# Two-block network with a 64-expert layer, one core: output norm and stores placed ahead of the last expert set, whose 128 tokens are gathered, normed as one tile and scattered

## The chip, the cores and the metric

The kernel runs on one core of a Trainium2 chip, in one launch. Five engines take part, each with its own instruction stream that it works through in order: PE (matrix multiply), DVE (VectorE), ACT (ScalarE), POOL (GpSimd) and SP (SyncE, which here only issues DMAs). The metric is the device time of one execution in microseconds (us); lower is better. Matrix products write PSUM, which DVE and ACT read; everything else on the chip lies in SBUF.

## The reference, cut to what matters

The first block and the mixing half of the second block are untouched here. What matters is the end of the second block: a two-level mixture of experts over 1024 tokens of width 1024, added to the scaled input, and a layer norm.

```python
g_sel = top_k(x @ w_rg + b_rg, 1)                  # one group of 8 experts
top_v, top_i = top_k(logits of that group, 2)      # two experts of 64 for each token
weights = g_w * softmax(top_v)
ffn = sum over the token's two experts e of
      weight * ((silu(x @ w1[e]) * (x @ w3[e])) @ w2[e])      # w1, w3: 1024x512, w2: 512x1024
out = layer_norm(ALPHA * x + ffn, ln2_g, ln2_b)    # over the 1024 columns, eps 1e-5
```

## The kernel before, in words

The tokens of each expert are padded to a capacity and put into columns of 128 places. The experts are worked off in 30 sets (`ORDER`): a set of kind Q holds four experts of 32 places, S one expert of 128 places, and so on. The last three sets are 27 (S), 28 (S) and 29 (Q). For a set, `weights` issues the loads of its expert weights on SP's queue (three pieces of 2 MB for each expert: two halves of w1 and w3 together, then w2; for a Q set w2 comes in 16 loads of 512 KB, four for each expert), `hidden` forms pg and pu over eight steps of k and the product h (L1997 to L2005), and `rows` turns h, multiplies by w2 (py, L2022) and scales by the routing weight.

The weights stand in a ring of eight 2 MB buffers (`E.chunk`). A new load waits until the buffer's last reader is done. The last set needs 12 loads; its four w2 loads take the buffers of its own first four, so they can be issued only when the first half of its `hidden` (k of 0 to 3) has been multiplied.

For the sets up to 26 the rows of `rows` go out by an indirect DMA to y_d, two rows for each token. The last three sets are not stored: their rows are kept as a high and a low part (yh, yl, `split_scaled`, L183 and L184), and `spread` adds them to the 8 token tiles xr (128 tokens each, called K.xa in the code): a one-hot matrix S is made from the tokens' numbers (L2034), and for each tile two halves pa are multiplied from S, yh and yl (L2041, L2042) and added to xr by DVE (L2046). The spread of a set is worked in between the steps of the next set's `hidden`. The rows stored in y_d are fetched back by `add(c)` (L2098, four loads of two tiles, into four buffers of the same ring) and added to xr, the even tiles by DVE and the odd ones by POOL, two additions of 128x1024 each (L2102).

After the last set stands a loop, `further`, over experts that overflowed their capacity. Then the tail: the gain and bias of the norm are loaded as two rows broadcast to 128 partitions (L2136), and for each of the 8 tiles the spread of set 29 is multiplied, in most tiles with the tile itself added on PE through an identity (L2044), and the tile is normed in one of three ways (`LAST`, L2140 to L2166) that share the work between ACT, DVE and POOL, and stored on SP's queue (L2166). The recording layer orders each engine's instructions by its own plan; what it decided is shown below where the change speaks of it.

Of the kernel before, what the change touches and what calls it, by code (L numbers as in the profile page):

```python
# [27 lines left out]
NCOL = sum(CAP) // P  # L28
NOVF = 40
NLATE = 3  # L30
LAST = "qpfpffff"
# [1650 lines left out]
def route(tc, K, RT):  # L1682
# [207 lines left out]
    dve.tensor_copy(K.wtab, pw[:, :NC_])  # L1890


    K.nblk = RT("nblk", (1, 1), I32)
    dve.tensor_copy(K.nblk, oe[0:1, 63:64])
    e1, e2_ = N((64, 64)), N((64, 64))
    ec = ecol[:64]
    dve.tensor_scalar(e1, ob[:64], ec, None, op0=OP.is_le)
# [46 lines left out]
def experts(tc, I, K, out):  # L1944
# [64 lines left out]
    def rows(R, h, parts, w, between=lambda t, bank: None):  # L2009
# [18 lines left out]
        for j in range(2):  # L2028
            K.H.split_scaled(R[1][:, j], R[2][:, j], py[j], w)

    def spread(R, tok):

        S, yh, yl = R
        dve.tensor_scalar(S.rearrange("p a b -> p (a b)"), K.io, tok, None, op0=OP.is_equal)  # L2034

        def part(t, bank=PS, keep=False):
            o = S[:, t // 4, t % 4 * P:(t % 4 + 1) * P]
            ps = []
            for j in range(2):
                pa, x = bank("pa"), K.xa[t][:, hs[j]]  # L2040
                pe.matmul(pa, o, yh[:, j], start=True, stop=False)  # L2041
                pe.matmul(pa, o, yl[:, j], start=False, stop=not keep)  # L2042
                if keep:
                    pe.matmul(pa, ident, x, start=False, stop=True)  # L2044
                else:
                    dve.tensor_tensor(x, x, pa, op=OP.add)  # L2046
                ps.append(pa)
            return ps

        return part  # L2050

# [10 lines left out]

    col = lambda a, c: a[:, c:c + 1]

    def further():

        r = E.chunk(dt=F32R).rearrange("p (r a b) -> p r a b", a=2, b=512)
        r = [r[:, i] for i in range(3)]
        nb = nc.values_load(K.nblk[0:1, 0:1], min_val=0, max_val=NOVF)
        with tc.For_i(0, nb, 1) as it:  # L2070
            e = nc.sync.value_load(K.bexp[0:1, bass.ds(it, 1)], min_val=0, max_val=63)
            ix, fx = Z("ix", (P, 1), I32, bufs=1), Z("fx", (P, 2), bufs=1)
            for o, a in ((ix, K.xdx), (fx[:, 0:1], K.tokf), (fx[:, 1:2], K.wtab)):
                nc.sync.dma_start(o, a[:, bass.ds(it + NCOL, 1)])
            ws, = weights([e])
            parts = [(full, ws)]
            rows(r, hidden([turn(fetch(ix))], parts)[0], parts, fx[:, 1:2])
            add = spread(r, fx[:, 0:1])
            for t in range(8):
                add(t)  # L2080
# [1 line left out]
    def cols(rs):  # L2082
        return range(BASE[rs[0]] // P, BASE[rs[0]] // P + max(1, CAP[rs[0]] // P))

    nxt = lambda t, bank: None
# [7 lines left out]
    def add(c):  # L2093
# [5 lines left out]
        for j in range(2):  # L2099
            for k in range(2):  # L2100
                x = K.xa[2 * c + j]
                (dve, pool)[j].tensor_tensor(x, x, y[:, j, k], op=OP.add)  # L2102

    xs = K.xg
    xT = [turn(x, PS) for x in xs]
    for i, rs in enumerate(order):
        if i == len(order) - 1:
            for c in range(4):
                add(c)
        ws = weights(ids[i] if i < 2 else [expert_id(r) for r in rs], len(rs) in CUT)  # L2110
        n = P // len(rs)
        parts = [(slice(n * j, n * j + n), w) for j, w in enumerate(ws)]
        xs = [fetch(col(K.xdx, c)) for rs_ in order[i + 1:i + 2] for c in cols(rs_)]
        if i == 0:
            pool.memset(xg[1], 0.0)
            for t in range(8):
                pool.tensor_scalar(K.io[:, t * P:(t + 1) * P], K.io128, float(t * P), None, op0=OP.add)
            K.close_pool("q")
            E.grow()
        if i == n_late:  # L2120
            R = [S] + [K.A4(n, (P, 2, 512), F32R) for n in ("yh", "yl")]
        h = hidden(xT, parts, nxt)
        xT = [turn(x) for x in xs]
        for j, c in enumerate(cols(rs)):
# [12 lines left out]


    for t in range(8):
        x, kind = K.xa[t], LAST[t]  # L2140
        pa = nxt(t, (PS, PT)[t % 2], kind != "q")
        rv, rt = Z("zrv", (P, 1), bufs=2), Z("zrt", (P, 1), bufs=2)
        if kind == "f":
            sm, nm, ss = Z("zsm", (P, 2), bufs=2), Z("znf", (P, 1), bufs=2), Z("zss", (P, 1), bufs=2)
            for j in range(2):
                act.activation(x[:, hs[j]], pa[j], AF.Copy, accum_out=sm[:, j:j + 1])  # L2146
            dve.tensor_scalar(nm, sm[:, 0:1], sm[:, 1:2], -1.0 / D, op0=OP.add, op1=OP.mult)  # L2147
            act.activation(row[:, 2], x, AF.Square, bias=nm, accum_out=ss)  # L2148
            K.H.rstd_of(rv, ss, D, 1e-5, rt)
        else:  # L2150
            mv, nm, st = Z("zmv", (P, 2), bufs=2), Z("znm", (P, 1), bufs=2), Z("zst", (P, 2, 6), bufs=2)
            src = pa if kind == "p" else [x[:, h] for h in hs]
            for j in range(2):
                dve.bn_stats(st[:, j], src[j])
            dve.bn_aggr(mv, st)
            K.H.rstd_of(rv, mv[:, 1:2], 1, 1e-5, rt)
            dve.scalar_tensor_tensor(nm, mv[:, 0:1], -1.0, rv, op0=OP.mult, op1=OP.mult)
        if kind != "f":
            for j in range(2):
                act.activation(x[:, hs[j]], src[j], AF.Identity, scale=rv, bias=nm)  # L2160
            pool.tensor_tensor(x, x, row[:, 0], op=OP.mult)
            pool.tensor_tensor(x, x, row[:, 1], op=OP.add)
        else:
            dve.scalar_tensor_tensor(x, x, nm, row[:, 0], op0=OP.add, op1=OP.mult)  # L2164
            dve.scalar_tensor_tensor(x, x, rv, row[:, 1], op0=OP.mult, op1=OP.add)  # L2165
        nc.sync.dma_start(out[t * P:(t + 1) * P, :], x)  # L2166
    K.close_pool("e2")


# [64 lines left out]
```

## Time and profile before

| what | value |
|---|---|
| median of 3 runs | 3249.79 us (3246.05 to 3254.64) |
| the profiled execution | 3248.72 us |
| its span in the profile | 3246.8 us |
| busy share of the span: PE, DVE, ACT, POOL | 91%, 50%, 26%, 24% |
| HBM traffic over the span | 206 GB/s, in the expert phase about 420 GB/s |

The span is from the first to the last instruction that the profiler saw; the execution's own time is 1.9 us more, and the median is 1.1 us above that. Busy shares are means over stages with different limits, so the change is read from the last 130 us alone.

### The profile page before, as it was taken

The page shows a single profiled execution, that of the slowest core. Times are in us where ns is not written, and L with a number is a line of the kernel's source. Part 1 is how long each engine was busy: PE and PEld are TensorE (multiplying, and loading weights), DVE is VectorE, ACT ScalarE, POOL GpSimd, SP SyncE. Part 2 cuts the span into 40 slices and gives each one's busy share as a digit, 9 for nine tenths or more (in the row PEclk, how much of TensorE's full clock was granted, in tenths as well). Part 3 has the DMA queues.
Part 4 walks back from the last instruction along what each step waited for, and adds up shares of the span by engine and source line. Part 5 has one row for each costly group of instructions (what it writes and reads, how often), then busy time and mean ns, then how long its engine had stood idle before and what let it go on. Part 6 is the DMA issues. An engine that isn't in the chain of part 4 may idle for free. (4 is left out here: it accounts for less than half of the span.)

```text
span 3246.8 us, 39751 instructions
## 1 busy us (share of the span) xinstructions
PE 2970.0 (91%) x15247; PEld 2090.4 (64%) x15247; DVE 1635.0 (50%) x2700; ACT 847.3 (26%) x1474; POOL 768.1 (24%) x591
## 2 busy tenths in 40 slices
PE   7789989999999899999889999988989888989886
PEld 7789968888888678778778788963423322323232
DVE  7865495555566899885888544460000000000054
ACT  4233343333211533334332532120101100101002
POOL 4521174333200333333442142011000000000021
PEclk8899999999999899999999999988989999999998
DMA  3012222222622323313222575449999999999994
GB/s 122 18 45 100 79 78 79 88 87 97 240 88 91 117 91 105 110 67 109 66 62 71 175 238 174 170 195 414 390 422 396 422 416 414 427 400 425 386 426 190
DMA packets 135552, 656.54 MB, mean 202 GB/s; under 512 B 18693, under 2 KB 31877, under 8 KB 113728
## 3 DMA queue, kind: packets, MB, share of 16 engines
q1 hardware_dynamic: 119536, 615.75, 49.3%
q0 software_dynamic: 13520, 34.03, 2.7%
q10 hardware_dynamic: 2304, 4.20, 0.3%
q8 instruction: 121, 1.98, 0.3%
q14 instruction: 71, 0.58, 0.1%
HBM read 584.19 MB, written 85.46 MB: 206 GB/s over the span
## 5 line engine op out<-in xcount | busy, mean ns | idle before, releaser
L2005 DVE TENSOR_TENSOR h<-h,pu 128x512 f32<-128x512 f32 x32 | 22.0, 687 | 842.5 <-PE pu L1997 842.5
L1997 PE MATMUL pg<-w,xT 128*32 128x512 f32 (+2 forms) x1056 | 348.8, 633 | 76.7 <-DMA w<-in_we_dram 76.6
L1997 PE MATMUL pu<-w,xT 128*32 128x512 f32 (+2 forms) x1056 | 342.9, 622 | 0.0
L2022 PE MATMUL py<-w,hT 128*32 128x512 f32 (+2 forms) x1056 | 281.9, 599 | 15.5 <-issue 12.4
L1997 PEld LDWEIGHTS pg<-w,xT 128*32 128x32 f32 (+2 forms) x1056 | 96.0, 139 | 244.1 <-issue 128.3
L1997 PEld LDWEIGHTS pu<-w,xT 128*32 128x32 f32 (+2 forms) x1056 | 104.0, 140 | 168.9 <-issue 166.2
L2022 PEld LDWEIGHTS py<-w,hT 128*32 128x32 f32 (+2 forms) x1056 | 98.6, 135 | 166.8 <-issue 141.6
L321 POOL TENSOR_TENSOR ws<-wr 128x512 f32<-128x512 f32 x74 | 115.2, 1561 | 274.6 <-DMA wr<-in_w2T_dram 137.5
L1111 DVE TENSOR_TENSOR x<-x,pd 128x512 f32<-128x512 f32 x176 | 118.2, 685 | 76.2 <-PE pd L190 75.4
L180 DVE TENSOR_TENSOR ol<-ws,oh 128x512 fp32r<-128x512 f32 x148 | 123.6, 836 | 45.7 <-ACT oh L179 38.8
L2004 ACT ACTIVATE h<-pg 128x512 f32<-128x512 f32 x32 | 19.1, 597 | 484.9 <-PE pg L1997 462.0
L1678 POOL DMA_INDIRECT y_d<-y,ydx x29 | 29.0, 999 | 433.5 <-ACT y L2026 433.5
L179 ACT ACTIVATE oh<-ws 128x512 fp32r<-128x512 f32 x148 | 92.1, 626 | 141.0 <-PE pm L189 131.0
L1672 POOL DMA_INDIRECT xg<-x_d,xdx x31 | 31.6, 1020 | 402.5 <-PE pxg L1984 401.4
L189 PE MATMUL pd<-wdl,aoh 128*128 128x512 f32 x320 | 124.1, 392 | 0.0
L190 PE MATMUL pd<-wdh,aol 128*128 128x512 f32 x320 | 123.9, 391 | 0.0
L188 PE MATMUL pd<-wdh,aoh 128*128 128x512 f32 x320 | 121.5, 396 | 2.1 <-DVE b21l L184 2.1
L180 DVE TENSOR_TENSOR ol<-wr,oh 128x512 fp32r<-128x512 f32 x117 | 108.3, 927 | 5.1 <-ACT oh L179 2.8
L179 ACT ACTIVATE oh<-wr 128x512 fp32r<-128x512 f32 x117 | 72.9, 625 | 118.9 <-PE pm L189 110.0
L180 POOL TENSOR_TENSOR wl<-wrB,wh 128x512 fp32r<-128x512 f32 x40 | 60.0, 1522 | 181.8 <-ACT wh L179 181.8
L1213 DVE SCALAR_TENSOR_TENSOR cadve<-cadve,vec 128x512 f32<-128x512 f32 x105 | 102.1, 972 | 0.1
L1213 DVE SCALAR_TENSOR_TENSOR cudve<-cudve,vec 128x512 f32<-128x512 f32 x105 | 98.2, 936 | 0.8
(814 smaller groups left out, 7993.4 us busy)
## 6 DMA issues: line engine op xcount, KB each, us to landing
w<-in_we_dram SPq DMA_DIRECT2D x160, 2048.0 KB, 23.9
w<-in_we_dram SPq DMA_DIRECT2D x128, 512.0 KB, 10.3
wr<-in_w2T_dram SPq DMA_DIRECT2D x34, 512.0 KB, 4.1
wr<-in_wg_dram SPq DMA_DIRECT2D x22, 512.0 KB, 3.3
wr<-in_wu_dram SPq DMA_DIRECT2D x22, 512.0 KB, 4.1
act_d<-go SPq DMA_DIRECT2D x22, 512.0 KB, 2.9
wrD<-act_d SPq DMA_DIRECT2D x22, 512.0 KB, 3.3
wrD<-in_wd_dram SPq DMA_DIRECT2D x22, 512.0 KB, 4.4
```

The lines of the kernel that those rows point to most:

```text
L179: act.activation(hi, src, AF.Copy)
L180: (eng or dve).tensor_tensor(lo, src, hi.bitcast(F32), op=OP.subtract)
L188: pe.matmul(ps, l[0], r[0], start=(k == 0), stop=False)
L189: pe.matmul(ps, l[0], r[1], start=False, stop=False)
L190: pe.matmul(ps, l[1], r[0], start=False, stop=(k == n - 1))
L321: self.pool.tensor_tensor(s, self.s[a], self.s[b], op=op)
L1111: dve.tensor_tensor(xs, xs, pd, op=OP.add)
L1213: dve.scalar_tensor_tensor(o, x, w, c, op0=OP.mult, op1=OP.add)
L1672: nc.gpsimd.indirect_dma_start(out=x, out_offset=None, in_=K.x2d, in_offset=bass.IndirectOffsetOnAxis(ap=ix, axis=0), bounds_check=T - 1, ...
L1678: nc.gpsimd.indirect_dma_start(out=K.y2d, out_offset=bass.IndirectOffsetOnAxis(ap=ix, axis=0), in_=y, in_offset=None, bounds_check=2 * T - ...
L1997: pe.matmul(p[r], x[:, k, r], ws[k4][:, k % 4, j], start=(k == 0), stop=(k == 7))
L2022: pe.matmul(py[j][r], hT[:, k, r], ws[2][:, k, j], start=(k == 0), stop=(k == 3))
```

## The change

The sets, the routing and the weights stay. What moves is everything behind the last two sets.

- The spread of set 28 is no longer worked in between the steps of set 29's `hidden`. It runs in one piece right behind set 28's `rows`, in PSUM banks of both kinds in turn.
- Set 29 is not spread. Ahead of its `hidden`, its one-hot matrix S is turned on PE (pst, eight 128x128), and the finished token tiles are gathered by it on PE into px: 16 products of 128x512 in float32. A matrix `same` says which of the 128 places hold the same token. Behind set 29's `rows`, yh and yl times `same` are added to px (four products), and px is normed as one tile and scattered to the output by an indirect DMA on POOL's queue.
- All 8 tiles are normed (`norms`): statistics for four tiles at a time on DVE, then for each tile one pass on ACT into one of two buffers xg, a product with the gain on DVE, a sum with the bias on POOL and a store on POOL's queue. In the code this stands ahead of set 29's `hidden`. The tiles' rows that belong to set 29's tokens are overwritten by the scatter.
- Gain and bias (`row_load`) are loaded on SP's queue behind the loads of set 29's weights, into the buffers of K.io and of a turned input.
- `further` stands behind the scatter; a second loop, which runs at most once, repeats the spread of set 29 and the norms if there were overflowing experts.

```diff
+    def norms(ts):
+
+        n = len(ts)
+        mv = Z("zmv", (P, n, 2), bufs=2)
+        for i, t in enumerate(ts):
+            st = Z("zst", (P, 2, 6), bufs=2)
+            for j in range(2):
+                dve.bn_stats(st[:, j], K.xa[t][:, hs[j]])
+            dve.bn_aggr(mv[:, i], st)
+        rv, nm = Z("zrv", (P, n), bufs=2), Z("znm", (P, n), bufs=2)
+        K.H.rstd_of(rv, mv[:, :, 1], 1, 1e-5, Z("zrt", (P, n), bufs=2))
+        dve.scalar_tensor_tensor(nm, mv[:, :, 0], -1.0, rv, op0=OP.mult, op1=OP.mult)
+        for i, t in enumerate(ts):
+            o = xg[t % 2]
+            act.activation(o, K.xa[t], AF.Identity, scale=rv[:, i:i + 1], bias=nm[:, i:i + 1])
+            dve.tensor_tensor(o, o, row[0], op=OP.mult)
+            pool.tensor_tensor(o, o, row[1], op=OP.add)
+            nc.gpsimd.dma_start(out[t * P:(t + 1) * P, :], o)
...
+        if last:
+
+            tok = col(K.tokf, cols(rs)[0])
+            one_hot(R[0], tok)
+            row = [K.io, xTs[turned[0] % 2].rearrange("p k t -> p (k t)")]
+            row_load()
+            same = Z("same", (P, P), F32R)
+            ST = []
+            for j in range(2):
+                pq = PT("pst")
+                for t in range(4):
+                    pe.transpose(pq[:, t * P:(t + 1) * P], S[:, j, t * P:(t + 1) * P].bitcast(F32), ident)
+                ST.append(Z("h", (P, 512), bufs=2))
+                act.activation(ST[j], pq, AF.Copy)
...
+            px = [PS("px") for _ in range(2)]
+            for t in range(8):
+                for j in range(2):
+                    pe.matmul(px[j], ST[t // 4][:, t % 4 * P:(t % 4 + 1) * P], K.xa[t][:, hs[j]], start=(t == 0), stop=False)
+            norms(range(4))
+            norms(range(4, 8))
         h = hidden(xT, parts, nxt)
+        nxt = none
         xT = [turn(x) for x in xs]
+        if last:
+            act.activation(Z("zsq", (P, 1)), tok, AF.Sqrt)
...
-                nxt = spread(R, col(K.tokf, c))
-    further()
-    row = E.chunk().rearrange("p (a d) -> p a d", d=D)
-    for i in range(2):
-        nc.sync.dma_start(row[:, i], bass.AP(tensor=I["rows4"].tensor, offset=i * D, ap=[[0, P], [1, D]]))
...
+                if not last:
+                    nxt = spread(R, col(K.tokf, c))
+        if i == len(order) - 2:
+            for t in range(8):
+                nxt(t, (PS, PT)[t % 2])
+            nxt = none
+
+
+    st, mv, rv = Z("lst", (P, 2, 6)), Z("lmv", (P, 2)), Z("lrv", (P, 1))
+    for j in range(2):
+        for y in R[1:]:
+            pe.matmul(px[j], same, y[:, j], start=False, stop=(y is R[2]))
+        dve.bn_stats(st[:, j], px[j])
+    dve.bn_aggr(mv, st)
+    x = xg[1]
+    for j in range(2):
+        dve.scalar_tensor_tensor(x[:, hs[j]], px[j], mv[:, 0:1], row[0][:, hs[j]], op0=OP.subtract, op1=OP.mult)
+    K.H.rstd_of(rv, mv[:, 1:2], 1, 1e-5, Z("lrt", (P, 1)))
+    for j in range(2):
+        dve.scalar_tensor_tensor(x[:, hs[j]], x[:, hs[j]], rv, row[1][:, hs[j]], op0=OP.mult, op1=OP.add)
+    nc.gpsimd.indirect_dma_start(out=out, out_offset=bass.IndirectOffsetOnAxis(ap=col(K.xdx, cols(order[-1])[0]), axis=0), in_=x, in_offset=None,
+                                 bounds_check=T - 1, oob_is_err=False)
```

Where DVE's order changes first: before, around the end of set 28's `hidden`. L2046 adds a spread half from PSUM, L2102 a fetched row, L2005 is the product h of set 28, L184 its low part yl, L2034 a one-hot matrix.

```order
L2046 TENSOR_TENSOR xr<-xr,pa 128x512 x4
L2102 TENSOR_TENSOR xr<-xr,w 128x1024 x2
L2046 TENSOR_TENSOR xr<-xr,pa 128x512 x2
L2005 TENSOR_TENSOR h<-h,pu 128x512
L2046 TENSOR_TENSOR xr<-xr,pa 128x512 x2
L2034 TENSOR_SCALAR S<-io,tokf 128x1024
L2016 COPY hT<-ph 128x256
L2017 COPY hT<-ph 128x256
L2102 TENSOR_TENSOR xr<-xr,w 128x1024 x4
L184 SCALAR_TENSOR_TENSOR yl<-py,wtab,yh 128x512 x2
L2046 TENSOR_TENSOR xr<-xr,pa 128x512 x16
L2034 TENSOR_SCALAR S<-io,tokf 128x1024
```

The same place on DVE now, with the line numbers of the changed file (L2052 was L2046, L2106 was L2102, L2038 was L2034, L183 was L184).

```order
L2052 TENSOR_TENSOR xr<-xr,pa 128x512 x14
L2005 TENSOR_TENSOR h<-h,pu 128x512
L2052 TENSOR_TENSOR xr<-xr,pa 128x512 x2
L2038 TENSOR_SCALAR S<-io,tokf 128x1024
L2016 COPY hT<-ph 128x256
L2017 COPY hT<-ph 128x256
L2164 COPY xg_18956<-tokf 128x128
L183 SCALAR_TENSOR_TENSOR yl<-py,wtab,yh 128x512 x2
L2052 TENSOR_TENSOR xr<-xr,pa 128x512 x16
L2106 TENSOR_TENSOR xr<-xr,w 128x1024 x8
L2038 TENSOR_SCALAR S<-io,tokf 128x1024
L2119 BN_STATS zst<-xr 128x6 x3
```

All eight additions of fetched rows now stand behind the sixteen of set 28's spread, where before all eight stood ahead of them, and the one-hot matrix of set 29 stands behind all of these.

On PE the steps of set 29's `hidden` (pg and pu with 32 rows) began right behind set 28's py, with pieces of the spread between them; before:

```order
L2022 MATMUL py<-w,hT 128x512 x8
L1997 MATMUL pg<-w,xT_19273 32x512
L1997 MATMUL pu<-w,xT_19273 32x512
L2041 MATMUL pa<-yh,S 128x512
L2042 MATMUL pa<-yl,S 128x512
L2041 MATMUL pa<-yh,S 128x512
L2042 MATMUL pa<-yl,S 128x512
```

On PE now, from the end of set 28's spread on:

```order
L2050 MATMUL pa<-yh,S 128x512
L2051 MATMUL pa<-yl,S 128x512
L2160 MATMUL pst<-ident,S 128x128 x8
L2166 MATMUL ptok<-ident,xg_18956 128x128
L2171 MATMUL px<-xr,h 128x512 x16
L1997 MATMUL pg<-w,xT_19274 32x512 x4
L1997 MATMUL pu<-w,xT_19274 32x512 x4
L1997 MATMUL pg<-w,xT_19274 32x512 x4
```

Set 29's `hidden` now stands behind the whole spread, the eight turns of S and the sixteen gathering products.

On DVE behind the last set's rows stood, before, the end of set 29 and the entry of the loop:

```order
L2005 TENSOR_TENSOR h<-h,pu 128x512
L2016 COPY hT<-ph 128x256
L2017 COPY hT<-ph 128x256
L184 SCALAR_TENSOR_TENSOR yl<-py,wtab,yh 128x512 x2
L2069 TENSOR_LOAD nblk
L2070 COMPARE_AND_BRANCH
```

On DVE now, from the yl of set 29 on; L2127 is the product of a normed tile with the gain, L2199 the statistics of px:

```order
L183 SCALAR_TENSOR_TENSOR yl<-py,wtab,yh 128x512 x2
L2127 TENSOR_TENSOR xg_18956<-xg_18956,io 128x1024
L2127 TENSOR_TENSOR xg_19273<-xg_19273,io 128x1024
L2199 BN_STATS lst<-px 128x6 x2
L2200 BN_AGGR lmv<-lst 128x2
L193 TENSOR_SCALAR lrt<-lmv 128x1
L196 RECIPROCAL lrv<-rsq 128x1
L197 TENSOR_TENSOR rsq<-lrv 128x1
L198 TENSOR_TENSOR rsq<-rsq,lrt 128x1
L199 TENSOR_SCALAR rsq<-rsq 128x1
L200 TENSOR_TENSOR lrv<-lrv,rsq 128x1
L2127 TENSOR_TENSOR xg_18956<-xg_18956,io 128x1024
```

Five more of L2127 follow, and then the four passes over px (L2203, L2206). So none of the eight products with the gain stands ahead of set 29's last rows. On SP the two loads of gain and bias stand behind all 24 loads of set 29.

## Rows read from the trace of the kernel before

**Rows 1.** Windows: stretches in us, then busy time (instructions) by engine, clock, DMA.

```profile
core 0: us, PE busy (x) PEld busy (x) DVE busy (x) ACT busy (x) POOL busy (x), PEclk, DMA share, GB/s
3120.00:3140.00 20.00, 16.44 (x50) 8.71 (x49) 17.60 (x16) 0.60 (x1) 15.69 (x6) 1.00 1.02 429
...
3220.00:3247.00 27.00, 4.23 (x13) 2.07 (x11) 22.31 (x46) 9.87 (x26) 8.85 (x4) 0.64 0.35 140
```

**Rows 2.** Timeline of SP's queue, 3040 to 3205: start, us, line, transfer.

```profile
3119.11 32.97 SPq L1937 DMA_DIRECT2D w<-in_we_dram  x8
3174.02 14.91 SPq L1967 DMA_DIRECT2D w<-in_we_dram  x16
3202.62 0.82 SPq L2136 DMA_DIRECT2D w<-in_rows_dram  x2
```

**Rows 3.** Waits of SP's queue, 3040 to 3250: total us, times, longest.

```profile
SPq L1967 <- PE pu L1997: 30.1, 4, 21.8
```

**Rows 4.** Timeline of all engines around set 28, 3120 to 3152.

```profile
3133.02 5.99 DVE L2102 TENSOR_TENSOR xr<-xr,w 128x1024 f32<-128x1024 f32 x2
3135.58 1.02 PE L1997 MATMUL pu<-w,xT 128*128 128x512 f32 x2
3140.12 0.67 DVE L2005 TENSOR_TENSOR h<-h,pu 128x512 f32<-128x512 f32 x1
3143.05 7.13 PE L2022 MATMUL py<-w,hT 128*128 128x512 f32 x16 [0.88 <-DVE hT L2016]
3151.55 0.74 DVE L184 SCALAR_TENSOR_TENSOR yl<-py,wtab,yh 128x512 fp32r<-128x512 f32 x1
```

**Rows 5.** The lines L2102 and L2046: ns minimum/median/maximum of one, first and last start.

```profile
L2102 POOL TENSOR_TENSOR xr<-xr,w x8: 2357/3001/3327, 3121.7 to 3144.9; 128x1024 f32<-128x1024 f32 x8
L2102 DVE TENSOR_TENSOR xr<-xr,w x8: 1211/2702/3431, 3124.2 to 3150.4; 128x1024 f32<-128x1024 f32 x8
L2046 DVE TENSOR_TENSOR xr<-xr,pa x34: 673/686/690, 3117.7 to 3204.7; 128x512 f32<-128x512 f32 x34
```

**Rows 6.** Timeline of PE, ACT and DVE: a cold start, set 29's first half, float32 products, one-hot.

```profile
3090.56 1.91 PE L1997 MATMUL pg<-w,xT 128*128 128x512 f32 x2 [3.00 <-DMA w<-in_we_dram]
3095.80 1.02 PE L1997 MATMUL pg<-w,xT 128*128 128x512 f32 x2
3141.56 0.60 PE L2013 MATMUL ph<-ident,h 128*128 128x128 f32 x4
3141.92 0.74 DVE L2034 TENSOR_SCALAR S<-io,tokf 128x1024 fp32r<-128x1024 f32 x1
3167.78 1.07 PE L1997 MATMUL pg<-w,xT 128*32 128x512 f32 x8
3173.81 1.10 PE L1997 MATMUL pu<-w,xT 128*32 128x512 f32 x8
```

**Rows 7.** Timeline at the end of set 29 and the start of the tail.

```profile
3200.62 1.61 DVE L184 SCALAR_TENSOR_TENSOR yl<-py,wtab,yh 128x512 fp32r<-128x512 f32 x2 [15.87 <-ACT yh L183]
3202.96 0.50 PE L2041 MATMUL pa<-yh,S 128*128 128x512 f32 x1 [2.24 <-DVEq L2070]
```

**Rows 8.** Lines of ACT and POOL, a store's issue last: ns minimum/median/maximum.

```profile
L2148 ACT ACTIVATE w<-xr,znf x5: 1139/1147/1149, 3214.4 to 3237.6; 128x1024 f32<-128x1024 f32 x5
L2162 POOL TENSOR_TENSOR xr<-xr,w x3: 2349/2362/2370, 3215.7 to 3232.4; 128x1024 f32<-128x1024 f32 x3
L1659 POOL DMA_DIRECT2D x_d<-xr x8: 531/532/630, 2097.3 to 2151.7; - x8
```

**Rows 9.** DMA issues: queue, count, KB each, median us to landing; stores on POOL's queue first.

```profile
x_d<-xr POOLq DMA_DIRECT2D x8, 512.0 KB, 2.9
out_dram<-xr SPq DMA_DIRECT2D x8, 512.0 KB, 2.6
y_d<-y,ydx POOLq DMA_INDIRECT x7, 10.5
```

**Rows 10.** The last instruction that the timeline of the tail shows.

```profile
3243.00 0.33 SPq L2166 DMA_DIRECT2D out_dram<-xr  x1
```

More of the change, by code (lines that the diff above doesn't have):

```diff
@@ L1890, in route @@
     dve.tensor_copy(K.wtab, pw[:, :NC_])
[L1893 to L1894 removed]
+    K.nblk = RT("nblk", (1, 2), I32)
+    dve.tensor_copy(K.nblk[:, 0:1], oe[0:1, 63:64])
+    dve.tensor_scalar(K.nblk[:, 1:2], oe[0:1, 63:64], 1.0, None, op0=OP.min)
     e1, e2_ = N((64, 64)), N((64, 64))
@@ L2029, in rows, with places, one_hot, part @@
             K.H.split_scaled(R[1][:, j], R[2][:, j], py[j], w)
+    def places(again=True):
+        if again:
+            nc.sync.dma_start(K.io[:, 0:P], I["cmoe"][:, 8:8 + P])
+        for t in range(again, 8):
+            pool.tensor_scalar(K.io[:, t * P:(t + 1) * P], K.io[:, 0:P] if again else K.io128, float(t * P), None, op0=OP.add)
+    def one_hot(S, tok):
+        dve.tensor_scalar(S.rearrange("p a b -> p (a b)"), K.io, tok, None, op0=OP.is_equal)
     def spread(R, tok):
         S, yh, yl = R
-        dve.tensor_scalar(S.rearrange("p a b -> p (a b)"), K.io, tok, None, op0=OP.is_equal)
-        def part(t, bank=PS, keep=False):
+        if tok is not None:
+            one_hot(S, tok)
+        def part(t, bank=PS):
             o = S[:, t // 4, t % 4 * P:(t % 4 + 1) * P]
-            ps = []
             for j in range(2):
@@ L2041, in part @@
                 pe.matmul(pa, o, yh[:, j], start=True, stop=False)
[L2042 to L2048, printed above, removed]
+                pe.matmul(pa, o, yl[:, j], start=False, stop=True)
+                dve.tensor_tensor(x, x, pa, op=OP.add)
         return part
@@ L2083, in cols @@
         return range(BASE[rs[0]] // P, BASE[rs[0]] // P + max(1, CAP[rs[0]] // P))
-    nxt = lambda t, bank: None
+    none = nxt = lambda t, bank: None
     ids = [[expert_id(r) for r in rs] for rs in order[:2]]
@@ L2102, in add, with row_load @@
                 (dve, pool)[j].tensor_tensor(x, x, y[:, j, k], op=OP.add)
+    def row_load():
+        for k in range(2):
+            nc.sync.dma_start(row[k], bass.AP(tensor=I["rows4"].tensor, offset=k * D, ap=[[0, P], [1, D]]))
+    def norms(ts):
[15 more added lines that the diff above has]
+            nc.gpsimd.dma_start(out[t * P:(t + 1) * P, :], o)
     xs = K.xg
@@ L2106, in experts @@
     for i, rs in enumerate(order):
-        if i == len(order) - 1:
+        last = i == len(order) - 1
+        if last:
             for c in range(4):
@@ L2115, in experts @@
             pool.memset(xg[1], 0.0)
-            for t in range(8):
-                pool.tensor_scalar(K.io[:, t * P:(t + 1) * P], K.io128, float(t * P), None, op0=OP.add)
+            places(False)
             K.close_pool("q")
@@ L2121, in experts @@
             R = [S] + [K.A4(n, (P, 2, 512), F32R) for n in ("yh", "yl")]
+        if last:
[11 more added lines that the diff above has]
+                act.activation(ST[j], pq, AF.Copy)
+            tb = xg[0][:, 0:P]
+            dve.tensor_copy(tb, tok.to_broadcast([P, P]))
+            pq = PT("ptok")
+            pe.transpose(pq[:, 0:P], tb, ident)
+            dve.tensor_scalar(same, pq[:, 0:P], tok, None, op0=OP.is_equal)
+            px = [PS("px") for _ in range(2)]
[4 more added lines that the diff above has]
+            norms(range(4, 8))
         h = hidden(xT, parts, nxt)
+        nxt = none
         xT = [turn(x) for x in xs]
+        if last:
+            act.activation(Z("zsq", (P, 1)), tok, AF.Sqrt)
         for j, c in enumerate(cols(rs)):
@@ L2131, in experts @@
                 rows(R, h[j], parts, col(K.wtab, c), *[nxt] * (j > 0))
-                nxt = spread(R, col(K.tokf, c))
-    further()
-    row = E.chunk().rearrange("p (a d) -> p a d", d=D)
-    for i in range(2):
-        nc.sync.dma_start(row[:, i], bass.AP(tensor=I["rows4"].tensor, offset=i * D, ap=[[0, P], [1, D]]))
[L2139 to L2166, printed above, removed]
@@ L2167, in experts @@
+    further(nb)
+    with tc.For_i(0, nr, 1):
+        places()
+        add = spread(R, tok)
+        for t in range(8):
+            add(t)
+        row_load()
+        for t in (0, 4):
+            norms(range(t, t + 4))
     K.close_pool("e2")
```

7 lines of the change are left out of this document (4 added, 3 removed).

## The prediction, made before the changed kernel ran

> **What bounds the kernel now.** I read the windows of the last 130 us first, then SP's queue, then the timeline from set 28 on. While sets run, the DMA engines are full (share 1.02 from 3120 to 3140), and behind the last set DVE is: it is busy 22.3 of the last 27 us, with PE at 4.2 [rows 1]. SP shows how the two parts meet. The sixteen w2 loads of set 29 start at 3174.02, and SP had waited for PE's pu for 21.8 us at the longest [rows 2, 3]: they need the buffers that the first half of set 29's `hidden` frees. Those 8 MB set the end of the set: yl is done at 3200.62 + 1.61 = 3202.2 [rows 7]. From there to the span's end at 3246.8 the tail takes 44.6 us. So two distances decide: from set 28 to the first w2 load, and from the last yl to the end. The change is meant to shorten the second one; I work out both.
>
> **From set 28 to the first w2 load.** Up to about 3121 nothing differs. Then DVE is rid, for the moment, of the additions of fetched rows (L2102). Before, two of them (5.99 us) stood ahead of the last spread halves, and h of set 28 was formed at 3140.1 though PE had ended pu at 3136.6 [rows 4]. Now h comes some 3.6 us earlier, so py runs from about 3139.4 to 3146.5, and yl of set 28 is done at about 3148.0 (the two yl at 0.74 us behind the two yh, as in the row) [rows 4].
>
> Then DVE adds set 28's spread in one piece: 16 halves of 0.686 us [rows 5] are 11.0 us, and PE, with eight PSUM banks in turn, keeps up: 3148.6 to 3159.6. Only then come DVE's eight additions of fetched rows, which write the same tiles; POOL's eight can start when tile 1 is done, four halves in, at 3151.3. In the trace one of these takes POOL 2.36 us at best and 3.00 in the median, DVE 1.21 at best and 2.70 in the median [rows 5]: where both run, each is stretched by the other. Taken as excluding each other they need 8 x 2.36 + 8 x 1.21 = 28.6 us from 3151.3: 3179.9. Taken as independent DVE would end at 3159.6 + 9.7 = 3169.3 and POOL at 3151.3 + 18.9 = 3170.2. The medians lie near the first (2.70 is nearer to 1.21 + 2.36 = 3.57 than to 1.21), so I take 3179.9 and keep 3170.2 as the lower bound.
>
> The Trainium skill ("SBUF — State Buffer", section "SBUF: two separate sides") says that a DVE instruction with two SBUF inputs and a GpSimd instruction take turns on one pair of ports, the later one blocked for the whole of the other. By that rule the sum is 3179.9, without it 3170.2, and the stretched medians agree with the rule.
>
> One more instruction of DVE stands in between, the one-hot of set 29 (0.74 us [rows 6]), done at 3180.6. PE has by then been idle for 20 us. It turns S: 0.60 us for four transposes [rows 6], about double for its first few us, since PE behind a wait of 3.0 us took 1.91 us for a pair of products that takes 1.02 five us later [rows 6]. With ACT's first copy (0.6 us, half of a pass over 1024 columns [rows 8]) the gathering starts at about 3182.9. Its 16 products of 128x512 in float32 cost what the eight of py do, 7.13 us for eight [rows 4], so 14.3, and about 0.7 for the rest of the cold start less the overlap of their ends: 3197.6. Only then does set 29's `hidden` begin. Its first half is not held by data: its four loads wait for set 28's buffers alone and land in the 3150s. Its last pu begins 6.03 us after its first pg [rows 6], so the first w2 load goes out at about 3203.8 instead of 3174.0: **29.8 us later**. The lower bound, from independent additions, is 20; the upper 33, with POOL's median in place of its best for the four or five additions that overlap.
>
> The second four loads of set 29 now wait for the fetched rows' buffers, freed between about 3171 and 3180. At 429 GB/s [rows 1], 4.9 us for 2 MB, they have landed by 3193, ahead of the second half of `hidden` at 3204.5: no cost, with 11 us of cover. The w2 loads themselves, set 29's second half, its h, py and yl take what they took before, 28.2 us from the first w2 load to the end of yl: yl is done at **3232.0**.
>
> **From the last yl to the end.** The statistics of all tiles and the first two passes on ACT lie ahead of set 29's h, under its matmuls, and cost nothing: from the one-hot at 3180.6 to the end of `hidden` at about 3211 DVE has 30 us, and its sixteen statistics, at the 0.69 us of a pass over 512 columns, are 11. But none of the eight products with the gain stands there. The rows they need are loaded behind the last of set 29's loads on SP's queue, and DVE's order puts all eight behind yl; DVE works in order, so they cannot start earlier even if the rows did come. With two buffers xg, each tile passes through: ACT 1.15 us, DVE 1.21 (as L2102's best, the same shape), POOL 2.36, the store 2.9 until it has landed, about 0.4 for four handovers: 8.0 us for a round of two tiles [rows 5, 8, 9]. The first round has ACT's part done: two DVE products (2.4), two POOL sums with the store's issue between them (2.36 + 0.53 + 2.36), the store (2.9) and 0.3: 10.9 us until tile 1 is stored. Three more rounds are 24.0: 34.9. px is ready early in that time, but DVE's four passes over it write the buffer of tile 7 and stand behind its store: at 0.69 each, as L2046, 2.8 in all: 37.7.
>
> Then the scatter. Before, nothing is scattered with idle DMA engines. Plain stores of as many bytes land after 2.6 to 2.9 us, indirect ones under full load after 10.5 in the median [rows 9]. The tail's DMA engines are little used (share 0.35 before [rows 1]), so I take 4.5, near the plain store with a microsecond more for the issue. Two loop entries follow, 0.73 us each from yl to PE's next instruction [rows 7], and the end, which before lay 3246.8 - 3243.0 - 2.6 = 1.2 us behind the landing of the last store [rows 9, 10]. In all 37.7 + 4.5 + 1.5 + 1.2 = **44.9 us**, bounds 41 (handovers free, the scatter like a store) and 52 (the scatter at 10.5).
>
> So the tail is as long as the old one, 44.6, and it begins 29.8 us later. Span: 3232.0 + 44.9 = 3276.9; the profiled execution takes 1.9 us more than its span: 3278.8, which is 30.1 above the profiled 3248.7; on top of the median of 3249.8 that is **3280 us**, 0.9% slower. A change of less than 0.3%, about 10 us, could not be told from none here.
>
> **The rivals.** *Independent additions (11%)*: DVE and POOL do not hold each other up once DVE's additions stand in one piece. The medians of L2102 speak against it. The shift is 20 and the time about 3270.
>
> *Slow stores (13%)*: the eight stores and the scatter, now on POOL's queue, land later than 2.9 because DVE's products hold up their issue, or the scatter takes 10.5. For it: no POOL store of the trace was made between DVE products of this kind. Three rounds longer by 1.2 (one DVE product each) and the scatter's 6 make 10 us: 3290. [...]
>
> *The norm is covered after all (6%)*: the other side. If the eight products, sums and stores did run while the w2 loads are under way, the tail would be the four passes over px with the chain of small instructions (some 5 us), scatter, loops and end, about 12 us instead of 44.9, and even with the shift the time would be 3280 - 33 = 3247. It decides itself at one point: whether DVE's first product with the gain starts before yl of set 29. The printed order says no.
>
> *PE's gathering is covered by earlier data (2%)*: if the shift were below 10, the time would stay under 3260. That needs the additions done by 3160, against DVE's own 9.7 us behind the spread.
>
> **How the numbers follow.** My forecast, 3272 to 3287, has 68%. With independent additions 11, slow stores 13, the covered norm 6 and the small shift 2. Slower by over 0.3%: 92%. Within 0.3%: the small shift and most of the covered norm, 6%. Faster: 2%. The range leaves out the two last cases and the far end of slow stores: 3266 to 3292.
>
> **What would show it.** Right: DVE's sixteen spread halves in one run from about 3148; additions of DVE and POOL stretched, ending near 3180; a PE gap of about 20 us ahead of the turns of S; the first w2 load near 3204; all eight products with the gain behind yl near 3232, with a store to wait for in each round of about 8 us; a scatter at about 3270. Wrong: a gain product ahead of yl, additions that end near 3170, the gathering at well under 0.8 us a product, or rounds of under 6 us.

## The result, and the profile after

The changed kernel takes 3277.8 us, the median of five runs (3272.8 to 3284.9), against 3249.8 for the kernel before beside it, also of five. The ratio is 1.0092 (95% interval 1.0079 to 1.0105): slower, as forecast, 2 us below the forecast 3280 and inside its range. The profiled execution takes 3276.9 us, 28.2 more than that of before.

All distances below are counted from one instruction that both kernels share, the first yl of set 27. In the timeline of DVE it starts here before:

```profile
3115.40 0.75 DVE L184 SCALAR_TENSOR_TENSOR yl<-py,wtab,yh 128x512 fp32r<-128x512 f32 x1 [6.83 <-ACT yh L183]
```

and 6.3 us earlier in the changed kernel. Its timeline from there to the gathering on PE (start, duration, engine, line, wait before it):

```profile
3109.05 0.75 DVE L183 SCALAR_TENSOR_TENSOR yl<-py,wtab,yh 128x512 fp32r<-128x512 f32 x1 [6.83 <-ACT yh L182]
...
3139.41 1.61 DVE L183 SCALAR_TENSOR_TENSOR yl<-py,wtab,yh 128x512 fp32r<-128x512 f32 x2 [6.62 <-ACT yh L182]
3140.94 9.81 DVE L2052 TENSOR_TENSOR xr<-xr,pa 128x512 f32<-128x512 f32 x16
3143.66 23.57 POOL L2106 TENSOR_TENSOR xr<-xr,w 128x1024 f32<-128x1024 f32 x8 [60.14 <-DVE xr L2052]
3150.67 19.92 DVE L2106 TENSOR_TENSOR xr<-xr,w 128x1024 f32<-128x1024 f32 x8
3170.51 0.74 DVE L2038 TENSOR_SCALAR S<-io,tokf 128x1024 fp32r<-128x1024 f32 x1
3171.30 1.97 PE L2160 MATMUL pst<-ident,S 128*128 128x128 f32 x8 [23.98 <-DVE S L2038]
3173.28 15.31 PE L2171 MATMUL px<-xr,h 128*128 128x512 f32 x32
```

The sixteen spread halves stand in one piece, the additions of fetched rows (L2106) behind them, and PE waits 24.0 us for S before it turns it and gathers (the count x32 is of two passes for each float32 product). Only then comes `hidden` of set 29, and SP's queue shows what that does to the weights:

```profile
3195.60 14.89 SPq L1967 DMA_DIRECT2D w<-in_we_dram  x16
3212.55 0.34 SPq L2110 DMA_DIRECT2D io<-in_rows_dram  x1
3213.84 0.34 SPq L2110 DMA_DIRECT2D xT<-in_rows_dram  x1
```

The first w2 load goes out 86.6 us behind the mark, before it was 58.6 [rows 2]. The rows of gain and bias (L2110) come last. The windows of the end, with columns as in [rows 1], show both halves of the loss:

```profile
3140.00:3160.00 20.00, 7.27 (x31) 5.55 (x30) 19.82 (x22) 0.24 (x1) 16.10 (x6) 0.81 0.36 122
3160.00:3180.00 20.00, 8.70 (x22) 4.98 (x23) 20.00 (x29) 2.68 (x4) 7.15 (x3) 0.60 0.94 384
3180.00:3200.00 20.00, 20.00 (x128) 7.31 (x131) 3.28 (x17) 2.48 (x3) 0.00 (x0) 1.00 0.22 69
...
3230.00:3275.00 45.00, 0.00 (x0) 0.00 (x0) 13.23 (x11) 7.44 (x6) 21.62 (x16) 0.50 0.23 95
```

From 3140 to 3180 DVE is full and PE is busy for 16 of the 40 us and waits for the other 24, from 3180 to 3200 PE is full and the DMA engines have a share of 0.22, and in the last 45 us no engine is full: DVE is busy for 13 and POOL for 22. That last stretch is a chain, as the timeline shows:

```profile
3224.81 2.35 DVE L2127 TENSOR_TENSOR xg<-xg,io 128x1024 f32<-128x1024 f32 x2
...
3232.95 0.59 POOL L2129 DMA_DIRECT2D out_dram<-xg  x1 [0.30 <-POOL xg L2128]
...
3235.98 1.24 ACT L2126 ACTIVATE xg<-xr,znm,zrv 128x1024 f32<-128x1024 f32 x1 [2.03 <-DMA out_dram<-xg]
3237.25 1.46 DVE L2127 TENSOR_TENSOR xg<-xg,io 128x1024 f32<-128x1024 f32 x1 [2.05 <-ACT xg L2126]
3238.80 2.33 POOL L2128 TENSOR_TENSOR xg<-xg,xT 128x1024 f32<-128x1024 f32 x1 [0.31 <-DVE xg L2127]
3243.53 0.57 POOL L2129 DMA_DIRECT2D out_dram<-xg  x1 [2.40 <-issue]
...
3259.99 0.56 POOL L2129 DMA_DIRECT2D out_dram<-xg  x1 [0.30 <-POOL xg L2128]
3262.99 1.41 DVE L2203 SCALAR_TENSOR_TENSOR xg<-px,lmv,io 128x512 f32<-128x512 f32 x2 [5.72 <-DMA out_dram<-xg]
3264.31 1.41 DVE L2206 SCALAR_TENSOR_TENSOR xg<-xg,lrv,xT 128x512 f32<-128x512 f32 x2
3266.01 1.02 POOL L2207 DMA_INDIRECT out_dram<-xg,xdx  x1 [5.46 <-DVEq L2073]
```

One buffer can be followed in it: its store goes out at 3232.95, ACT takes the buffer again at 3235.98 (it had waited for the store), then DVE, then POOL, and the next store is at 3243.53. The two stores after that in this buffer are 8.2 us apart, which is the round that the prediction built. The first gain product starts behind yl of set 29 (done at 3224.9), and the span ends at 3274.9.

### The profile page after: what moved, and what is told of

It is laid out like the page before. It is cut to its first block, busy times and chain, and to the rows that moved or that the text cites. A ratio compares the mean times of both kernels' runs of the same rounds, so it can differ in the third digit from the quotient of the medians.

```text
span 3274.9 us, 39798 instructions
## 1 busy us (share of the span) xinstructions
PE 2950.6 (90%) x15232; PEld 2086.5 (64%) x15232; DVE 1633.4 (50%) x2685; ACT 845.6 (26%) x1447; POOL 777.4 (24%) x602
## 5 line engine op out<-in xcount | busy, mean ns | idle before, releaser
L2005 DVE TENSOR_TENSOR h<-h,pu 128x512 f32<-128x512 f32 x32 | 22.0, 688 | 850.1 <-PE pu L1997 830.2
L2022 PE MATMUL py<-w,hT 128*32 128x512 f32 (+2 forms) x1056 | 278.8, 598 | 15.2 <-issue 12.4
```

Source lines behind the costliest of these rows:

```text
L2022: pe.matmul(py[j][r], hT[:, k, r], ws[2][:, k, j], start=(k == 0), stop=(k == 3))
```

## The experiments

Two theories stood against each other. Mine: 28 us are lost ahead of the first w2 load, because the additions and the gathering stand in front of set 29's `hidden` on DVE and PE, and the tail did not get shorter because the products with the gain stand behind yl, their rows being loaded last. The rival: the norm cannot be put under the w2 loads, whatever the order, because stores and loads need the same DMA engines or the same in-order queues. Besides, the price of the additions and of the two buffers was to be settled. This table has all kernels (distances from the mark, taken from the profiled execution; "first w2 load" is its issue, "tail" is the end less yl):

| kernel | median us | ratio to before (95%) | first w2 load | yl 29 done | tail | end |
|---|---|---|---|---|---|---|
| before | 3249.8 | | 58.6 | 86.8 | 44.6 | 131.4 |
| changed | 3277.8 | 1.0092 (1.0079–1.0105) | 86.6 | 115.8 | 50.0 | 165.9 |
| rows early | 3257.1 | 1.0032 (1.0021–1.0043) | 86.6 | 125.0 | 18.8 | 143.8 |
| additions first | 3266.2 | 1.0050 (1.0033–1.0066) | 76.5 | 106.0 | 50.0 | 156.1 |
| gathering late | 3277.2 | 1.0088 (1.0072–1.0105) | 78.3 | 112.2 | 50.0 | 162.2 |
| four buffers | 3271.8 | 1.0076 (1.0059–1.0093) | 86.9 | 116.5 | 41.3 | 157.8 |
| additions on DVE | 3261.3, one run | | 84.2 | 123.2 | 18.6 | 141.8 |
| four buffers, sums on DVE | 3262.1 | 1.0042 (1.0028–1.0057) | 87.0 | 116.5 | 34.3 | 150.8 |
| all causes undone | 3242.0 | 0.9987 (0.9976–0.9997) | 63.8 | 116.8 | 15.2 | 132.0 |
| and half of set 29 first | 3232.6 | 0.9953 (0.9933–0.9974) | 47.9 | 98.4 | 19.5 | 117.9 |
| and sums on DVE | 3223.0 | 0.9936 (0.9922–0.9951) | 49.5 | 96.2 | 15.5 | 111.6 |

The kernel before, run beside the experiments, had medians of 3247.5, 3246.6 and 3246.2 us, and the ratios of the experiments are to these; the changed kernel's is to the 3249.8 of its own comparison. The intervals reach 0.1 to 0.2% (3 to 7 us) to either side, so differences of a few us between two medians are not clear of noise; the distances are of one execution each.

**The rows early.**

```diff
-    def weights(es, by_k=False):
+    def weights(es, by_k=False, mid=None):
...
+            if mid and i == 2:
+                mid()
...
+        if last:
+            tok = col(K.tokf, cols(rs)[0])
+            one_hot(R[0], tok)
+            row = [K.io, xTs[turned[0] % 2].rearrange("p k t -> p (k t)")]
-        ws = weights(ids[i] if i < 2 else [expert_id(r) for r in rs], len(rs) in CUT)
+        ws = weights(ids[i] if i < 2 else [expert_id(r) for r in rs], len(rs) in CUT, row_load if last else None)
```

> Only the load of the two rows (gain and bias) moves: on SP's queue from behind the last w2 load of set 29 to ahead of the first. With that DVE's order has two of the eight products with the gain ahead of h of set 29 and the other six ahead of yl. My theory is that the tail was not shortened because these products stood behind yl: then products, sums and stores run under the w2 loads, the tail from yl to the end falls from 50.0 us to 15 to 20, the 4 MB of stores cost the 8 MB of loads up to 10 us, and the time is 3243 to 3256. Rival: the products cannot use that time, because the stores and the w2 loads need the same DMA engines and each byte stored early is a byte loaded late, or because products ahead of h hold up the set: then yl comes as much later as the tail gets shorter, and the time is 3265 or more.

The edit also writes the one-hot of set 29 earlier in the code, but it runs where it did, 61.5 us from the mark in both kernels, so what moved in time is the load of the rows. The tail fell to 18.8 us as my theory has it, but yl came 9.2 us later, so the gain is 22 us in the profile and the median, 3257.1, lies 1 us above my band. ACT's timeline shows what took the rest:

```profile
3198.18 1.28 ACT L2006 ACT_TABLE_LOAD   x1 [17.02 <-PE pg L1999]
3199.47 0.60 ACT L2006 ACTIVATE h<-pg 128x512 f32<-128x512 f32 x1
3199.96 2.36 ACT L2128 ACTIVATE xg<-xr,znm,zrv 128x1024 f32<-128x1024 f32 x2
3213.15 1.24 ACT L2128 ACTIVATE xg<-xr,znm,zrv 128x1024 f32<-128x1024 f32 x1 [10.82 <-DMA out_dram<-xg]
...
3226.68 1.24 ACT L2128 ACTIVATE xg<-xr,znm,zrv 128x1024 f32<-128x1024 f32 x1 [3.51 <-DMA out_dram<-xg]
3227.82 1.25 ACT L182 ACTIVATE yh<-py,wtab 128x512 fp32r<-128x512 f32 x2
```

The third pass stands behind the Silu of set 29 (h) and so idles with it for 17 us, a store beside the w2 loads holds up the fifth for 10.8 us, and yh of set 29 stands behind the last pass, so PE waited 6.1 us between the last py product, ended at 3222.4, and px. Of the 9.2 us, 2.6 lie ahead of that end (the w2 loads landed 2.6 us later, with stores under way beside them) and the rest in ACT's order. Both theories hold a part: the order kept the norm out of the covered time, and in-order ACT takes some of it back.

**The additions first.** `add(c)` moves back ahead of set 28's spread; nothing else.

```diff
-        if last:
-            for c in range(4):
-                add(c)
...
         if i == len(order) - 2:
+            for c in range(4):
+                add(c)
             for t in range(8):
                 nxt(t, (PS, PT)[t % 2])
```

> Only the additions of the fetched rows move: back ahead of the spread of set 28, where the kernel before had them. My theory: the 19.9 us that they take on DVE behind the spread are on the path to the first w2 load; back under set 28's matmuls they delay yl of set 28 by 3 to 4 us and then cost nothing, PE waits for S some 10 us in place of 24.0, the first w2 load comes 13 to 15 us earlier, the tail stays at 48 to 50 us, and the time is 3261 to 3267. Rival: the gathering on PE, or the buffers that the w2 loads need, come late anyway: less than 4 us, 3274 or more.

PE's wait for S is 4.7 us and no longer 24.0, and the first w2 load comes 10.0 us earlier:

```profile
3165.77 1.97 PE L2157 MATMUL pst<-ident,S 128*128 128x128 f32 x8 [4.72 <-DVE S L2038]
3167.75 15.91 PE L2168 MATMUL px<-xr,h 128*128 128x512 f32 x32
```

The additions cost set 28 more than the 3 to 4 us I allowed: its yl is done at 3154.3, 40.2 us from the mark instead of 32.0 (37.6 in the kernel before), so 8 of the 20 us were not free there either, and 1.6 more went into gaps of the spread and a slower gathering. The 10 us that are left show in the end one for one (165.9 to 156.1). The time is in my band, though the first w2 load came 10 us earlier and not 13 to 15.

**The gathering late.** The products into px and the norms are written behind `hidden` of set 29.

```diff
+        h = hidden(xT, parts, nxt)
+        if last:
             px = [PS("px") for _ in range(2)]
...
             norms(range(4, 8))
-        h = hidden(xT, parts, nxt)
```

> Only the 16 gathering products (with the norms) are written behind the hidden part of set 29. In PE's order the first half of that part then has five of the 16 products ahead of it and not 16; the turning of S stays ahead of most of it. My theory: eleven products at 0.96 us, 10.5 us, leave the path to the first w2 load, yl comes 10 us earlier, the tail stays, and the time is 3265 to 3270. Rival: PE's gathering is not on the path, since the w2 loads wait for something else: within 3 us of the changed kernel.

A miss: the median did not move, 3277.2 against 3277.8 (from the mark the end is 3.6 us earlier). That is the rival's number, but not its reason, since the first w2 load did wait for the gathering and came 8.2 us earlier. But the eleven products reappear on PE between the matmuls of `hidden`:

```profile
3191.84 1.13 PE L2173 MATMUL px<-xr,h 128*128 128x512 f32 x2
...
3194.74 4.56 PE L2173 MATMUL px<-xr,h 128*128 128x512 f32 x10
...
3201.06 4.56 PE L2173 MATMUL px<-xr,h 128*128 128x512 f32 x10
...
3214.51 0.66 PE L2013 MATMUL ph<-ident,h 128*128 128x128 f32 x4 [1.90 <-DVE h L2005]
```

h now comes 23 us behind the first w2 load, where it was 9 in the changed kernel, and yl is only 3.6 us earlier. I had taken the first w2 load to set yl; it does so only while PE has h ready before the weights land.

**Four buffers.**

```diff
+            oc = E.chunk().rearrange("p (a d) -> p a d", d=D)
+            ob = xg + [oc[:, 0], oc[:, 1]]
...
-            o = xg[t % 2]
+            o = ob[t % 4]
```

> Only the buffers of the norm change: four in turn in place of two (two of them are a weights' buffer that has come free). A round of two tiles is now 8.2 us because ACT waits for the store. If DVE's product (1.21) and POOL's sum (2.36) exclude each other, two tiles need 7.1 us and the issue of two stores comes on top, so four buffers give back 1 us or less a round: a tail of 46 to 49 us, 3274 to 3277. If they run side by side, POOL alone sets the pace, 5.8 us for two tiles with the issue of their stores: a tail of 41 us, 3268 to 3270.

The tail is 41.3 us, the number that I had put down to engines that run side by side, and the time, 3271.8, lies between my two bands. The rows of the products and sums (ns minimum/median/maximum) say otherwise:

```profile
L2127 DVE TENSOR_TENSOR w<-w,io x4: 1218/2560/3380, 3226.5 to 3245.4; 128x1024 f32<-128x1024 f32 x4
L2128 POOL TENSOR_TENSOR w<-w,xT x4: 2347/2834/3344, 3232.0 to 3250.4; 128x1024 f32<-128x1024 f32 x4
```

They do stretch each other, to 3.38 and 3.34 us, but only two of DVE's eight products were stretched that far: two took 1.7 to 1.8 us and four 1.22, in the time in which POOL issues stores or waits. So the wait for a store's landing was worth 8.7 us of the tail, and my expectation had tied two questions into one that do not hang together.

**All additions on DVE**, to see what stretches them.

```diff
-                (dve, pool)[j].tensor_tensor(x, x, y[:, j, k], op=OP.add)
+                dve.tensor_tensor(x, x, y[:, j, k], op=OP.add)
```

> All sixteen additions of fetched rows are DVE's; POOL has none. They stay behind the spread. Asked is why DVE took 2.49 us for each of its eight in the changed kernel, and 1.21 at best. If DVE and POOL exclude each other, DVE alone needs 16 x 1.21 = 19.4 us from the end of the spread, and the additions end when they end now (19.9 us behind the spread). If DVE is slow for another reason, the weights that land in SBUF at the time, sixteen take 16 x 2.49 = 39.8 us. The total time is no part of this: with another estimate of the additions the order changes elsewhere too (two products with the gain stand ahead of h of set 29 although the rows are still loaded last), so it is likely to be slower, 3280 to 3300.

The line of the additions, in the changed kernel and then in this one (ns minimum/median/maximum):

```profile
L2106 POOL TENSOR_TENSOR xr<-xr,w x8: 2344/3202/3317, 3143.7 to 3164.0; 128x1024 f32<-128x1024 f32 x8
L2106 DVE TENSOR_TENSOR xr<-xr,w x8: 1210/3355/3356, 3150.7 to 3169.4; 128x1024 f32<-128x1024 f32 x8
```

```profile
L2106 DVE TENSOR_TENSOR xr<-xr,w x16: 1212/1215/1216, 3159.4 to 3176.5; 128x1024 f32<-128x1024 f32 x16
```

Without POOL every addition takes DVE 1.21 us, all sixteen 18.3, while the same weights land (the DMA engines moved 277 GB/s in that stretch, 212 during DVE's additions in the changed kernel). So it is POOL that stretches them, and POOL's help is worth nothing here: sixteen on DVE alone are done 18.3 us behind the spread, eight on each 19.9. Of the total I was wrong: with the additions estimated otherwise the rows went out ahead of the w2 loads, the tail fell to 18.6 us, and the kernel behaves like the one with the rows early.

**Four buffers and the bias sums on DVE.**

```diff
-            pool.tensor_tensor(o, o, row[1], op=OP.add)
+            dve.tensor_tensor(o, o, row[1], op=OP.add)
```

> The run with four buffers, with the eight sums of the bias on DVE and not on POOL. If the two engines exclude each other, a tile costs 1.21 + 2.36 = 3.57 us on the two as they stand and 2.42 on DVE alone: all eight are done 19.4 us behind yl, and the tail falls from 41.3 to 33 to 36 us, 3264 to 3267. If they do not, POOL's 2.36 and its issue of 0.55 are what a tile costs now, 2.9, and the gain is at most 4 us.

34.3 us of tail, the first case, and 3262.1 us, 2 under its band. DVE runs almost without a pause, and the stores issued meanwhile land after 2.9 to 3.4 us, against 2.9 to 3.0 in the changed kernel.

**All causes undone.** Additions first, spread of set 28 between set 29's matmuls again, one-hot, gathering and norms behind `hidden`, rows loaded from POOL's queue, four buffers.

```diff
         if i == len(order) - 2:
-            for t in range(8):
-                nxt(t, (PS, PT)[t % 2])
-            nxt = none
+            for c in range(4):
+                add(c)
...
+        h = hidden(xT, parts, nxt)
         if last:
             tok = col(K.tokf, cols(rs)[0])
...
-            nc.sync.dma_start(row[k], ...)
+            nc.gpsimd.dma_start(row[k], ...)
```

> All of the found causes undone together: additions ahead of set 28's spread, the spread between the matmuls of set 29's hidden part as in the kernel before, one-hot, gathering and norms written behind that part, the two rows loaded from POOL's queue as soon as the one-hot is made, four buffers. Counted from the first yl of set 27, the kernel before has its first w2 load at 58.6 us and its end at 131.4, the changed one 86.6 and 165.9. My theory: first w2 load at 58 to 62, yl of set 29 at 88 to 98 because stores share the DMA engines, the eight tiles done meanwhile, end at 108 to 120: 3226 to 3238, faster than both. Rival from the run with the early rows: in-order queues (ACT's passes wait for buffers, and h and yh of set 29 stand behind them) hold up the set itself, and the end is at 125 or later: 3243 or more.

The rival's case, nearly to the number: the end is at 132.0 and the time 3242.0. The cause is on ACT:

```profile
3184.21 1.24 ACT L2126 ACTIVATE xg<-xr,znm,zrv 128x1024 f32<-128x1024 f32 x1 [10.93 <-DMA out_dram<-xg]
3190.63 1.24 ACT L2126 ACTIVATE xg<-xr,znm,zrv 128x1024 f32<-128x1024 f32 x1 [5.18 <-DMA out_dram<-xg]
...
3193.18 0.60 ACT L2004 ACTIVATE h<-pg 128x512 f32<-128x512 f32 x1
3193.68 0.59 ACT L2159 ACTIVATE h<-pst 128x512 f32<-128x512 f32 x1
3194.32 9.56 PE L2170 MATMUL px<-xr,h 128*128 128x512 f32 x16 [18.18 <-ACT h L2159]
...
3205.80 7.13 PE L2170 MATMUL px<-xr,h 128*128 128x512 f32 x16
3212.87 7.07 PE L2022 MATMUL py<-w,hT 128*32 128x512 f32 x62
```

PE had ended set 29's `hidden` at 3176.1. Its Silu, and behind it ACT's copy of the turned S (L2159), stand behind two passes that wait for buffers whose stores, beside the w2 loads, land after up to 9.0 us. PE idles for 18.2 us until that copy, and the gathering, which it could have done in this time, then stands ahead of most of py, though the last w2 load had landed at 94.8 from the mark and py's main part begins at 108.2. So yl, done at 116.8, is as late as in the changed kernel although the first w2 load is 23 us earlier.

**And half of set 29 first.** The same, with set 28's spread held on PE until the first half of set 29's `hidden` is through.

```diff
+            def nxt(t, bank):
+                if t >= 4:
+                    with tc.issue_after(K.half.ins):
+                        sp(2 * t - 8, PT), sp(2 * t - 7, PT)
```

> As the run before, and PE does the first half of set 29's hidden part ahead of set 28's spread. The w2 loads wait for that half alone: first w2 load at 45 to 50 us from the first yl of set 27, yl of set 29 at 78 to 90. The norms still need the spread, now 7 us later: their stores end at 98 to 106 as before, and they, not the set, decide the end: 108 to 118, 3226 to 3236, within 6 us of the run before. Rival: the loads are what decides, then this one is 10 us or more faster than the run before.

3232.6 us, 0.5% faster than before. The first w2 load is at 47.9 and the end at 117.9, both as expected, but yl is at 98.4, and the lead over the run before is 9.5 us in the medians, not under 6. In ACT's order the Silu now stands ahead of all passes, and h, done at 72.1 in place of 89.8, no longer waits for stores. The loads are not what yl waited for in either run: here the last one had landed at 82.9, and py began at 85.2 and ended at 92.3, with the gathering between h and py on PE, and yh then waited for one more pass on ACT. Nor did the early issue bring the weights in earlier than before: the first w2 load, issued at 47.9 and at 58.6, landed at 62.6 in both, and the last but one at 81.6 and 82.2. From its issue to its landing here the DMA engines were full with earlier loads (share 1.00, 410 GB/s).

**And the sums on DVE**, with the norms written behind set 29's `rows`, which puts its copies of hT ahead of six of the eight tiles.

```diff
-            norms(range(4))
-            norms(range(4, 8))
...
+                if last:
+                    norms(range(4))
+                    norms(range(4, 8))
...
-            pool.tensor_tensor(o, o, row[1], op=OP.add)
+            dve.tensor_tensor(o, o, row[1], op=OP.add)
```

> The run with the first half of set 29 ahead of the spread, with the bias sums on DVE and the norms written behind set 29's py, which puts the copies of hT ahead of six of the eight tiles on DVE. There a tile took 3.5 us on DVE and POOL together, and the last store was issued 103 us from the first yl of set 27. With 2.42 us a tile on DVE alone the eight need 19.4 us in place of 28, yl stands right behind them, and the end comes 5 to 8 us earlier: 3224 to 3228. Rival: yl of set 29, in DVE's order behind all sixteen passes, is held up as much as the tiles gain, or the DMA engines set the pace of the stores: 3231 or more.

3223.0 us, 1 under my band, 0.64% faster than before, and 55 us under the changed kernel's median. The timeline shows the norm where the change wanted it, between the w2 loads and yl:

```profile
3156.71 23.66 SPq L1967 DMA_DIRECT2D w<-in_we_dram  x16
...
3182.74 2.36 DVE L2129 TENSOR_TENSOR xg<-xg,io 128x1024 f32<-128x1024 f32 x2
...
3199.76 2.35 DVE L2130 TENSOR_TENSOR w<-w,xT 128x1024 f32<-128x1024 f32 x2
3202.03 1.40 DVE L183 SCALAR_TENSOR_TENSOR yl<-py,wtab,yh 128x512 fp32r<-128x512 f32 x2
...
3209.41 1.01 POOL L2215 DMA_INDIRECT out_dram<-xg,xdx  x1 [6.47 <-DVEq L2075]
```

## Why the prediction was right, step by step

**The distance to the first w2 load** was right. It grew by 27.9 us (86.55 less 58.62), forecast 29.8. Set 28's yl was done 32.0 us from the mark; the spread halves took 9.8 (forecast 11.0); the additions, from POOL's first to DVE's last, 26.9 (28.6). That the two engines exclude each other, which the prediction took from stretched medians [rows 5], beside the rule of the Trainium skill ("SBUF — State Buffer", section "SBUF: two separate sides"), is now shown by a run: 3.36 us an addition beside POOL, 1.21 without, with sixteen on DVE done sooner than eight on each. It is nearly a full exclusion: while both add, DVE's additions start every 3.28 us, where one of DVE and one of POOL behind each other would be 1.21 + 2.35 = 3.56. The rival of independent additions falls. PE's gap was 24.0 us, the turns of S behind it 1.97 (from 3171.3 to 3173.3 the granted clock was 0.50, the lower of its two levels, 1.2 GHz, after PE had been idle for those 24 us), the gathering 15.3 (14.3 and 0.7).

**From the first w2 load to yl** it took 29.3 us, forecast 28.2.

**The tail** was the term that was mis-sized: 50.0 us where the sum had 44.9. The first round until tile 1 was stored took 11.1 (10.9) and the passes over px 2.7 (2.8). The three rounds took 27.0 and not 24.0: a round is 8.2, ACT's pass 1.24 and not 1.15, and once POOL waited 2.40 us more before a store for nothing that the profile shows. From the scatter's issue to the end it was 8.8 us, where 4.5 for the scatter, 1.5 for the loop entries and 1.2 at the end had 7.2. The scatter itself was not the long part: SP's wait for it ended 3.2 us behind its issue, and it landed after 3.2 us in the five kernels whose traces have the landing. What was too small were the loop entries and the end, 5.6 us and not 2.7. The step on order held: no gain product ahead of yl. The run with the rows early shows the reason too, since moving that one load put them ahead of it and took 31 us off the tail.

**Slow stores** did not come: where the trace has the landing, in six of the eight, it took 2.9 to 3.0 us, as POOL's plain stores did before [rows 9]; in the run with four buffers and the sums on DVE, where DVE hardly paused, it took 3.4 us at most. The Trainium skill ("SBUF — State Buffer", section "SBUF: two separate sides") has a trap in which a DMA issued from GpSimd waits for its descriptors while DVE runs an operation in a 2-port mode. The products here are two-input float32 tensor_tensor, and no such wait showed beside them.

**The offset.** The three terms make 27.9 + 1.1 + 5.4 = 34.4 us, and the spans differ by 28.1. The other 6.3 lie ahead of the mark, in stretches of which the prediction said that nothing differs. Of these, 3.7 are there at 2183.6 us already, up to which PE and ACT work through the same instructions in both kernels, so they are scatter between executions. The other 2.7 lie behind it, where ACT, DVE and POOL differ in a few small instructions (a Sqrt on ACT at 2187.0 stands in the changed kernel alone). From there to the mark the kernel before took 931.8 us and the ten others 928.4 to 932.4, so whether any of the 2.7 is the change's stays open. The mark itself lies between 3104.7 and 3118.0 in kernels whose instructions are the same up to there. The close hit of the total, 2 us, owes something to luck: a tail underestimated by 5 us was offset by an early mark and by a shift that was forecast 2 us too long.

## What to carry to other kernels

Work that is recorded under a stage of loads is covered only if every operand it needs, down to two rows of constants, is loaded ahead of that stage's own loads, and if no in-order engine has the stage's critical instruction behind it: here moving two small loads was worth 21 us, and a Silu and a copy behind passes that wait for stores, with the gathering that this pushed in front of py, ate up a lead of 23 us. A piece of work that leaves the end must not go in front of what starts the last loads; ask of the last loads which matmul frees their buffers, and put that first, but only as far as the DMA engines are not full with other loads at that time: the w2 load issued 10.7 us earlier than in the kernel before landed no earlier. Where DVE and GpSimd add or multiply two float32 tiles of SBUF each at the same time, sharing the work between them can be slower than giving it all to DVE (19.9 against 18.3 us for sixteen additions).

## What was unexpected of the hardware

Stores of 512 KB from POOL's queue land after 2.9 us in idle time but after up to 9.0 us beside the w2 loads, and any buffer that is reused behind them inherits that. One store of POOL's queue was held for 2.40 us without a visible cause in the changed kernel and in those with the rows early, the additions first, the gathering late and the additions on DVE, always the fourth store; with all causes undone, where the two rows go ahead on the same queue, it was the second, for 2.39. In these six it is the fourth plain transfer on the queue since the last rows went to y_d. With the rows early DVE was idle in those 2.40 us, so it is no work of DVE's; what it is was not found, and in the four other kernels, with another order on POOL, no such wait stands by itself. And from the issue of the indirect scatter of 128 rows to the end of the program it took 8.8 to 9.5 us in all these kernels, of which the scatter's landing was 3.2 where the trace has it.
